# A hybrid encoder block in three-matmul f32: eight products in some projection pieces, a residual added by the store, one more step ahead of a broadcast

## The chip, the cores and the metric

The kernel runs on one core of a Trainium2 chip. The metric is the time of one execution on the device in microseconds (us), lower is better. The engines are named as in the profile: PE is TensorE (matmul), PEld its weight loads, DVE is VectorE, ACT ScalarE, POOL GpSimd and SP SyncE. SP and ACT issue plain DMAs; POOL issues the DMAs that add to their destination.

## The reference, cut to what matters

The input is 512 tokens of 2048 features in f32.

```
hn = rmsnorm(h, g_mix); proj = hn @ w_in + b_in       # q k v o i f, cb cc ch, gm gc
hm = mlstm_chunkwise(q, k, v, i, f); ...; y_m = hm @ w_branch_m        # 1024 -> 2048
y_c = (cb * causal_dwconv(cc * ch)) @ w_branch_c                       # 1024 -> 2048
h  = h + (sigmoid(gm) * y_m + sigmoid(gc) * y_c) @ w_out               # 2048 -> 2048
hn = rmsnorm(h, g_ffn)
u  = causal_dwconv(hn @ w_up, w, b); gate, val = split(u)              # 2048 -> 2 x 5504
h  = h + (silu(gate) * val) @ w_down                                   # 5504 -> 2048
return rmsnorm(h, g_out)
```

## The kernel before, in words

Everything is held with features on the partitions and tokens along the row. An f32 product is made of three matmuls: each operand is split into a high part (ACT rounds it, `wh` for weights, `act[:, :NW]` for inputs) and a low part (DVE subtracts, `wl` and `act[:, NW:]`), and `three` in `cell_mm` issues high by high, high by low, low by high (L229, L230, L231).

The unit of work is an **item**: two blocks of 128 output features for all 512 tokens. Its sum over the input features goes in **pieces** of four 128-feature blocks, and a piece in two **cells**. A cell multiplies two by two weight blocks with two by two input blocks (two feature blocks, two halves of 256 tokens) by Winograd's form of Strassen's scheme: seven block products in place of eight, on sums of blocks. So a cell is 21 matmuls and a piece 42, each with 256 columns. The seventh product goes into bank 3 (`P_BANK`), which both items in flight share by halves, the other six into three banks of the item's set.

The sums cost work. Of a piece's weights, `fill` (L195) loads two blocks again and lets POOL add a third to each while loading (L204), and DVE makes two more sums (`s2` L169, `s4` L174). So a piece loads 512 KB plain, two plain copies of 128 KB, and adds two of 128 KB. ACT then makes two `wh` (`hi`, L184) and DVE two `wl` (`lo`, L188), 896 columns each. The inputs' seven slots are made by `cell_task` (L257): DVE sums L276, L281, L286, then high (L290) and low (L293), 1792 columns. When an item ends, `evac_first` (L245, ACT) takes bank 3's half into a buffer `z`, `evac_ops` (L251 to L254, DVE) puts the products together in it, and the item's `post` finishes it.

The phases follow one another: the input projection (40 items of 4 pieces), yc (8 items of 2 pieces), ym (8 of 2), out (8 of 4), up (43 of 4), down in three parts of its input features (8 items of 4, 3 and 3 pieces), and a short last part with plain products and the final norm. The first two and the last two items of a phase are interleaved piece by piece. One piece is one **step** of the main loop, and the program is written out step by step on all engines: in step s PE multiplies piece s, while DVE and ACT make the low and high parts of pieces s+1 and s+2 and the cells that `cells_at` puts there. A cell belongs to a whole phase, so at a phase's start four to eight new cells have to be made at once, beside the weights.

`post` work is put into a queue with a cost and is taken when the running `credit` of the step allows it; `flush(n)` forces what is still queued for items up to n. At an item's end the loop calls `flush(it.num - 3)`, then `evac_first`, and, when the item has a `pre` (a load of 512 KB for its post), `flush(it.num - 2)` and the load on SP. There are three buffers `z`, taken in turn (the order's names z_91, z_92, z_93), so `evac_first` of item n waits until the store of item n-3 has read its buffer.

In down, each part's `pre` loads the pair of h blocks, `residual` (L694, L695, DVE) adds and subtracts the sums, and ACT's queue stores the pair (L146), going from h_d to h2_d, back to h_d, and to h2_d. At out's end the squares' sum over features is made by `sum_tokens` (PE), `cols_post` (DVE, ends with L370) turns it into a diagonal, and `rows_pe` (PE, L373) broadcasts it over the partitions; these are queued as `side` stages, one per step: PE's part of a stage comes after the step's matmuls, its `post` part in the next step, ahead of that step's matmuls.

Of the kernel before, what the change touches and what calls it, by code (L numbers as in the profile page):

```python
# [49 lines left out]
class Item:  # L50


    def __init__(self, load, nq, xs, post, pre=None):
        self.load, self.nq, self.xs, self.post, self.pre = load, nq, xs, post, pre
        self.p1_start, self.urgent, self.done = True, False, False
        self.set = self.num = self.z = self.buf = None

# [11 lines left out]
def tile_block(ctx: ExitStack, tc: tile.TileContext, xT, w1, w_v0, w_v1, w_v2, w_bm, w_bc, w_out, w_up, w_down,  # L69
# [62 lines left out]
    gm_d, gc_d, mc_d, h_d, h2_d = (D_([KD, P, T], s) for s in ("gm_d", "gc_d", "mc_d", "h_d", "h2_d"))  # L132
# [16 lines left out]

    def pair_ap(d, a, b):  # L150

        return d[a:b + 1:b - a].rearrange("j p t -> p j t")
# [4 lines left out]

    def weight_task(it, q):
        t = Task(None, None, None, None)
# [46 lines left out]
    def tiles_load(w, n1, n2, k0=0):  # L206
        def load(raw, q):
            fill(raw, [w[n, :, k0 + 4 * q + i:k0 + 4 * q + i + 2, :] for n in (n1, n2) for i in (0, 2)])
# [12 lines left out]
    def cell_mm(it, q, r, t):  # L221
# [4 lines left out]
        def three(ps, ws, xs, start):  # L226
# [4 lines left out]
            PE.matmul(ps, l, xh, start=False, stop=last, skip_group_check=True)  # L231

        def p1():
            three(P_BANK[:, it.set * H2:(it.set + 1) * H2], *P1, first and it.p1_start)
# [22 lines left out]
    def cell_task(xs, c, d, scale=None, key=None):  # L257
# [7 lines left out]
        def load():  # L265
            new_raw()
            SP.dma_start(t.raw[:, 5 * SW:], d[k1])
            SP.dma_start(t.raw[:, :2 * SW], d[k2])

        def t3():  # L270
            x = slots(t.raw)
            if scale:
                A.activation(t.raw[:, 5 * SW:], t.raw[:, 5 * SW:], AF.Copy, scale=scale(k1))
                A.activation(t.raw[:, :2 * SW], t.raw[:, :2 * SW], AF.Copy, scale=scale(k2))
# [13 lines left out]
        def hi():  # L288
            t.act = actp.tile([P, 2 * NW], F32R, tag="act", name=nm("act"))
            A.activation(t.act[:, :NW], t.raw, AF.Copy)  # L290

        def lo():
            V.tensor_sub(t.act[:, NW:], t.raw, f(t.act[:, :NW]))  # L293
# [4 lines left out]
        t.load, t.sums, t.hi, t.lo, t.new_raw = load, [t3, e, t4], hi, lo, new_raw  # L298
        t.cost = (1.35, 1.95)
# [3 lines left out]
    def direct_cell(xs, c, it, d=None, scale=None, key=None):  # L303

        t = cell_task(xs, c, d, None, key)
# [9 lines left out]
        def t3():  # L315
            assert it.done
            a, b = t.raw[:, 5 * SW:], t.raw[:, :2 * SW]
# [11 lines left out]
        t.cost = (2.7, 1.95) if d is not None else t.cost  # L329
# [369 lines left out]
    def out_post(p):  # L699
        def post(it):  # L700
# [8 lines left out]
            def two_():  # L709
# [610 lines left out]
```

## Time and profile before

| | |
|---|---|
| three timed runs: median (lowest to highest) | 2734.19 us (2729.54 to 2740.98) |
| the profiled execution's own time | 2736.55 us |
| its span in the trace | 2734.8 us |
| PE, DVE, ACT, POOL busy | 94%, 81%, 47%, 31% |
| mean granted clock of PE | 0.978 |
| moved by DMA | 632.39 MB, mean 231 GB/s |

The PE matmuls of the page are pipelined, so their busy times overlap; the number of matmuls in a stretch says more. In the windows view each row is a stretch in us from the span's start, then its length, and for each engine the busy time and, in brackets, the number of instructions; then the granted clock, the DMA engines' mean busy share (packets overlap, so it can pass 1) and GB/s. The phases begin at 927.4 us (yc), 1035.3 (ym), 1131.4 (out), 1311.6 (up) and, for down's three parts, 2216.2, 2403.0 and 2538.0.

### The profile page before, as it was taken

The numbers are of one execution on the slowest core, as the hardware profiler recorded it, in microseconds if no ns is written. First come the engines' busy times: TensorE is split into PE (matmuls) and PEld (weight loads), VectorE is DVE, ScalarE is ACT, GpSimd is POOL, SyncE is SP. The second block draws the span as 40 slices with busy tenths as digits, with TensorE's granted clock in tenths as the row PEclk, the third lists the DMA queues.
The fourth block names the chain that finished last, engine by engine and source line by source line (L and its number), as shares of the span: only waits on it lengthen the run. The fifth ranks groups of instructions, "written<-read, shape, count | busy, mean of one in ns | idle before, by whom it ended". The sixth has DMA issues, their size and how long they took to land.

```text
span 2734.8 us, 55343 instructions
## 1 busy us (share of the span) xinstructions
PE 2582.4 (94%) x20860; PEld 2555.7 (93%) x20860; DVE 2214.5 (81%) x3376; ACT 1289.4 (47%) x1615; POOL 854.5 (31%) x1003
## 2 busy tenths in 40 slices
PE   7899999999999978899799999999999988989898
PEld 6899999999999978899699999999999988989897
DVE  5677776887677889978779988888888888787876
ACT  6444544445554434345545444444444444444443
POOL 3243333333333222232233333333333323232320
PEclk9999999999999999999899999999999999999998
DMA  7799988898999889898698888988888789899996
GB/s 191 176 235 234 242 230 225 218 240 235 239 238 228 229 252 268 227 269 242 181 226 212 227 220 220 229 217 226 219 221 227 204 217 263 234 288 260 275 266 200
DMA packets 499036, 632.39 MB, mean 231 GB/s; under 512 B 46496, under 2 KB 327072, under 8 KB 498768
## 3 DMA queue, kind: packets, MB, share of 16 engines
q1 hardware_dynamic: 323472, 446.01, 51.4%
q0 software_dynamic: 141536, 125.09, 31.0%
q10 hardware_dynamic: 33760, 57.76, 5.8%
q8 instruction: 163, 2.67, 0.4%
q14 instruction: 105, 0.86, 0.1%
HBM read 571.01 MB, written 57.67 MB: 230 GB/s over the span
## 4 chain that ended last, share of the span: by engine, by line
PE 75%; DVE 9%; DMA 7%; issue 3%; ACT 1%; POOL 0%; SPq 0%; DVEq 0%; ACTq 0%; POOLq 0%
PE bank L231 24%; PE bank L229 24%; PE bank L230 24%; DVE wl L188 3%; DMA raw<-in_w_down_dram 2%; DMA raw<-in_w_bc_dram 1%; DVE act L293 1%; DMA raw<-in_w_out_dram 1%; DMA h_d<-z 1%; DVE raw L169 1%; PE bank L542 1%; DMA raw<-in_w_up_dram 1%; DVE z L252 1%; DVE z L251 0%; DVE raw L174 0%
## 5 line engine op out<-in xcount | busy, mean ns | idle before, releaser
L231 PE MATMUL bank<-act,wl 128*128 128x256 f32 x6664 | 1909.4, 287 | 66.6 <-DVE wl L188 66.5
L229 PE MATMUL bank<-act,wh 128*128 128x256 f32 x6664 | 1915.7, 287 | 34.1 <-ACT z L245 19.0
L230 PE MATMUL bank<-act,wh 128*128 128x256 f32 x6664 | 1902.5, 285 | 0.6 <-DVE act L293 0.5
L184 ACT ACTIVATE wh<-raw 128x896 fp32r<-128x896 f32 x952 | 893.8, 951 | 1144.9 <-PE bank L230 715.6
L231 PEld LDWEIGHTS bank<-act,wl 128*128 128x128 f32 x6664 | 1296.6, 195 | 76.5 <-DVE wl L188 76.2
L229 PEld LDWEIGHTS bank<-act,wh 128*128 128x128 f32 x6664 | 1297.2, 195 | 40.7 <-ACT z L245 20.6
L230 PEld LDWEIGHTS bank<-act,wh 128*128 128x128 f32 x6664 | 1296.7, 195 | 4.3 <-issue 2.0
L188 DVE TENSOR_TENSOR wl<-raw,wh 128x896 fp32r<-128x896 f32 x952 | 1034.2, 1087 | 222.3 <-PE bank L231 156.1
L204 POOL DMA_DIRECT2D raw<-in_w_up_dram x344 | 299.3, 963 | 606.9 <-DMA raw<-in_w_up_dram 266.3
L204 POOL DMA_DIRECT2D raw<-in_w_dram x288 | 250.7, 944 | 550.6 <-DMA raw<-in_w_dram 300.4
L169 DVE TENSOR_TENSOR raw<-raw 128x256 f32<-128x256 f32 x476 | 199.6, 419 | 55.5 <-DMA raw<-in_w_down_dram 22.1
L204 POOL DMA_DIRECT2D raw<-in_w_down_dram x160 | 139.4, 973 | 309.3 <-DMA raw<-in_w_down_dram 119.8
L174 DVE TENSOR_TENSOR raw<-raw 128x256 f32<-128x256 f32 x476 | 199.0, 418 | 0.2
L290 ACT ACTIVATE act<-xraw 128x1792 fp32r<-128x1792 f32 x52 | 88.3, 1697 | 91.2 <-DVE xraw L286 91.1
L251 DVE TENSOR_TENSOR z<-bank,z 128x512 f32<-128x512 f32 x131 | 89.9, 686 | 19.2 <-ACT z L245 17.4
L293 DVE TENSOR_TENSOR act<-xraw,act 128x1792 fp32r<-128x1792 f32 x52 | 105.0, 2019 | 0.0
L584 DVE TENSOR_TENSOR z<-z,rstd 128x1024 f32<-128x1024 f32 x83 | 101.1, 1219 | 0.0
L204 POOL DMA_DIRECT2D raw<-in_w_out_dram x64 | 55.7, 966 | 125.8 <-DMA raw<-in_w_out_dram 91.5
L252 DVE TENSOR_TENSOR z<-bank,z 128x512 f32<-128x512 f32 x131 | 89.7, 684 | 0.8 <-DVE z L251 0.5
L254 DVE TENSOR_TENSOR z<-bank,z 128x512 f32<-128x512 f32 x131 | 89.6, 684 | 0.0
L245 ACT ACTIVATE z<-bank 128x256 f32<-128x256 f32 x131 | 48.2, 368 | 25.6 <-DMA h_d<-z 11.5
L253 DVE TENSOR_TENSOR z<-bank,z 128x256 f32<-128x256 f32 x131 | 55.6, 425 | 4.5
(208 smaller groups left out, 1209.6 us busy)
## 6 DMA issues: line engine op xcount, KB each, us to landing
raw<-in_w_up_dram SPq DMA_DIRECT2D x172, 512.0 KB, 5.9
raw<-in_w_dram SPq DMA_DIRECT2D x144, 512.0 KB, 5.8
raw<-in_w_up_dram SPq DMA_DIRECT2D x344, 128.0 KB, 4.4
raw<-in_w_up_dram POOLq DMA_DIRECT2D x344, 128.0 KB, 5.2
raw<-in_w_down_dram SPq DMA_DIRECT2D x80, 512.0 KB, 6.2
raw<-in_w_dram SPq DMA_DIRECT2D x288, 128.0 KB, 4.1
raw<-in_w_dram POOLq DMA_DIRECT2D x288, 128.0 KB, 5.2
raw<-in_w_down_dram SPq DMA_DIRECT2D x160, 128.0 KB, 4.7
```

Source lines behind the costliest of these rows:

```text
L169: V.tensor_add(x[:, 6], x[:, 5], x[:, 0])
L174: V.tensor_add(x[:, 2], x[:, 6], x[:, 1])
L184: A.activation(seven(t.wh[r]), half(r), AF.Copy)
L188: V.tensor_sub(seven(t.wl[r]), half(r), seven(f(t.wh[r])))
L204: G.dma_start(at(i), a21, accum_op=ALU.add)
L229: PE.matmul(ps, h, xh, start=start, stop=False, skip_group_check=True)
L230: PE.matmul(ps, h, xl, start=False, stop=False, skip_group_check=True)
L231: PE.matmul(ps, l, xh, start=False, stop=last, skip_group_check=True)
L251: return [lambda: V.tensor_add(z[:, 0:4:3], b0, two(z[:, 1])), lambda: V.tensor_add(z[:, 1:3], b1, two(z[:, 3])), lambda: V.tensor_add(z[: ...
L252: lambda: V.tensor_add(z[:, 1:3], b1, two(z[:, 3])),
L293: V.tensor_sub(t.act[:, NW:], t.raw, f(t.act[:, :NW]))
L584: V.tensor_mul(sb_pair(it.z), sb_pair(it.z), two(rstd))
```

## The change

Three edits.

**Eight products.** The last piece of each item of yc, ym and out (24 pieces) goes with the eight plain block products instead of seven: `eight_task` loads only the 512 KB, makes no sums, and takes high and low parts in 256-column halves, of 512 columns in all for each cell (the second output block with its sign turned, since the item's second half is kept negative). PE makes 48 matmuls for such a piece. The inputs of these pieces need six slots, made by one difference in place of three sums. As the shared bank gets nothing from that piece, its group of sums ends a piece earlier (`p1_end`). The costs that the planner reckons with are lower for them.

**Down's residual.** down's items have no `pre`. The post turns the second block's sign on ACT and the store becomes a DMA of POOL that adds the pair to h_d in place. h2_d is gone. The post's cost in the planner goes from 1.3 to 0.1.

**One more step.** A stage that does nothing stands between the squares' sum and the broadcast ahead of up.

```diff
+    def add_to(dst, src, key):
+        def fn():
+            G.dma_start(dst, src, accum_op=ALU.add)
+            stored.add(key)
+        late.append(fn)
...
+    def eight_task(it, q):
...
+        def hi(r):
+            w = t.wh[r] = wp.tile([P, NC], F32R, tag="wh", name=nm("wh"), bufs=4)
+            A.activation(at(w, 0), blk(0, r), AF.Copy)
+            A.activation(at(w, 1), blk(1, r), AF.Copy, scale=-1.0)
+
+        def lo(r):
+            w = t.wl[r] = wp.tile([P, NC], F32R, tag="wl", name=nm("wl"), bufs=3)
+            V.tensor_sub(at(w, 0), blk(0, r), at(f(t.wh[r]), 0))
+            V.scalar_tensor_tensor(at(w, 1), blk(1, r), -1.0, at(f(t.wh[r]), 1), op0=ALU.mult, op1=ALU.subtract)
...
+        t.load, t.sums, t.hi, t.lo = load, [], hi, lo
+        t.cost = (0, 1.5)
...
-            fill(raw, [w[n, :, k0 + 4 * q + i:k0 + 4 * q + i + 2, :] for n in (n1, n2) for i in (0, 2)])
+            if not eight:
+                fill(raw, [w[n, :, k0 + 4 * q + i:k0 + 4 * q + i + 2, :] for n in (n1, n2) for i in (0, 2)])
...
+        if q == it.eight:
+            for k in range(2):
+                for ws, xs, b, half in ((k, 2 * k, 0, 0), (k, 2 * k + 1, 2, 0), (2 + k, 2 * k + 1, 1, 1), (2 + k, 4 + k, 2, 1)):
+                    three(SETS[it.set][b][:, half * H2:(half + 1) * H2], ws, xs, False, last and k == 1)
+            return
...
-        t.load, t.sums, t.hi, t.lo, t.new_raw = load, [t3, e, t4], hi, lo, new_raw
-        t.cost = (1.35, 1.95)
+        t.load, t.sums, t.hi, t.lo, t.new_raw = load, [diff] if eight else [t3, e, t4], hi, lo, new_raw
+        t.cost = (0.65, 1.7) if eight else (1.35, 1.95)
...
                     side.append((lambda: sum_tokens(SIDE, acc, 1, 4, True, True), cols))
+                    side.append((noop, noop))
                     side.append((rows_pe, rows_post))
...
             def fn():
-                residual(it)
-                store(pair_ap((h2_d, h_d, h2_d)[c], j1, j2), sb_pair(it.z), ("d", c, p))
-            return [(1.3, fn)]
+                b = it.z[:, T:]
+                A.activation(b, b, AF.Copy, scale=-1.0)
+                add_to(pair_ap(h_d, j1, j2), sb_pair(it.z), ("d", c, p))
+            return [(0.1, fn)]
...
-            pre = load_pair((h_d, h2_d, h_d)[c], *kpair(p))
-            items.append(Item(tiles_load(w_down, *kpair(p), k0), nq, AA, down_post(c, p), pre))
+            items.append(Item(tiles_load(w_down, *kpair(p), k0), nq, AA, down_post(c, p)))
```

The orders of three places before and after follow, as the programs have them: line, operation, what is written from what, and its shape.

DVE in yc, where the third item's second piece gets its low parts (`wl`; `z` rows are an item's end, `raw` rows sums of weights), before:

```order
L169 TENSOR_TENSOR raw_10784<-raw_10784 128x256
L251 TENSOR_TENSOR z_92<-bank_84,z_92 128x2x256
L174 TENSOR_TENSOR raw_10784<-raw_10784 128x256
L252 TENSOR_TENSOR z_92<-bank_85,z_92 128x512
L253 TENSOR_TENSOR z_92<-bank_85,z_92 128x256
L188 TENSOR_TENSOR wl_10996<-raw_10778,wh_10918 128x896
L254 TENSOR_TENSOR z_92<-bank_86,z_92 128x512
L188 TENSOR_TENSOR wl_10999<-raw_10778,wh_10975 128x896
L169 TENSOR_TENSOR raw_10908<-raw_10908 128x256
L188 TENSOR_TENSOR wl_11049<-raw_10784,wh_10993 128x896
L174 TENSOR_TENSOR raw_10908<-raw_10908 128x256
L188 TENSOR_TENSOR wl_11054<-raw_10784,wh_11043 128x896
```

The same place on DVE now:

```order
L210 TENSOR_TENSOR raw_10767<-raw_10767 128x256
L301 TENSOR_TENSOR z_92<-bank_84,z_92 128x2x256
L215 TENSOR_TENSOR raw_10767<-raw_10767 128x256
L302 TENSOR_TENSOR z_92<-bank_85,z_92 128x512
L303 TENSOR_TENSOR z_92<-bank_85,z_92 128x256
L188 TENSOR_TENSOR wl_10987<-raw_10765,wh_10909 128x256
L189 SCALAR_TENSOR_TENSOR wl_10987<-raw_10765,wh_10909 128x256
L304 TENSOR_TENSOR z_92<-bank_86,z_92 128x512
L188 TENSOR_TENSOR wl_10991<-raw_10765,wh_10969 128x256
L189 SCALAR_TENSOR_TENSOR wl_10991<-raw_10765,wh_10969 128x256
L737 TENSOR_TENSOR z_91<-z_91,mA 128x1024
L229 TENSOR_TENSOR wl_11042<-raw_10767,wh_10984 128x896
```

Two subtractions of 896 columns, the first two `wl` rows of the upper list, became four of 256 (L188 and L189 in the lower), and the sums of the next such piece (L169 and L174 between the last `wl` rows of the upper list) are gone; yc's post (L737) has moved up into that place.

ACT in down's third part, from the end of its first item to the end of its third, before. `L245` is `evac_first`, `L184` makes a `wh` (two a step), and `L146` is a store, which goes out here in the order of ACT's queue:

```order
L146 DMA h_d<-z_91 128x2x512
L184 ACTIVATE wh_29367<-raw_29177 128x896
L184 ACTIVATE wh_29379<-raw_29183 128x896
L245 ACTIVATE z_91<-bank_83 128x256
L146 DMA h_d<-z_92 128x2x512
L184 ACTIVATE wh_29434<-raw_29183 128x896
L184 ACTIVATE wh_29446<-raw_29242 128x896
L184 ACTIVATE wh_29496<-raw_29242 128x896
L184 ACTIVATE wh_29508<-raw_29248 128x896
L184 ACTIVATE wh_29554<-raw_29248 128x896
L184 ACTIVATE wh_29566<-raw_29306 128x896
L245 ACTIVATE z_92<-bank_83 128x256
```

ACT at the same place now; `L813` is the sign turned ahead of POOL's add of the same buffer, `L295` is `evac_first`, `L225` makes a `wh`:

```order
L813 ACTIVATE z_91<-z_91 128x512
L295 ACTIVATE z_91<-bank_83 128x256
L225 ACTIVATE wh_29481<-raw_29236 128x896
L225 ACTIVATE wh_29493<-raw_29295 128x896
L225 ACTIVATE wh_29543<-raw_29295 128x896
L225 ACTIVATE wh_29555<-raw_29301 128x896
L225 ACTIVATE wh_29601<-raw_29301 128x896
L813 ACTIVATE z_92<-z_92 128x512
L813 ACTIVATE z_93<-z_93 128x512
L813 ACTIVATE z_91<-z_91 128x512
L225 ACTIVATE wh_29616<-raw_29359 128x896
L295 ACTIVATE z_92<-bank_83 128x256
```

The store of z_91 stood two `wh` ahead of the `evac_first` that writes the buffer anew, that of z_92 seven rows ahead; now the sign of z_91 is turned in the row just ahead of it, and that of z_92 four rows ahead, and the add comes after that. Without a `pre`, `flush(it.num - 2)` no longer forces the older item's post out at the item's end.

DVE at the start of down's first part, from the end of up's last posts but one: `L584` to `L743` are an up post, before:

```order
L743 TENSOR_TENSOR mB<-mB 128x512
L169 TENSOR_TENSOR raw_25837<-raw_25837 128x256
L251 TENSOR_TENSOR z_92<-bank_84,z_92 128x2x256
L174 TENSOR_TENSOR raw_25837<-raw_25837 128x256
L252 TENSOR_TENSOR z_92<-bank_85,z_92 128x512
L253 TENSOR_TENSOR z_92<-bank_85,z_92 128x256
L188 TENSOR_TENSOR wl_25991<-raw_25773,wh_25918 128x896
L254 TENSOR_TENSOR z_92<-bank_86,z_92 128x512
L188 TENSOR_TENSOR wl_25994<-raw_25773,wh_25976 128x896
L584 TENSOR_TENSOR z_91<-z_91,rstd 128x1024
L734 SCALAR_TENSOR_TENSOR mA<-z_91,pcol,mA 128x511
L735 SCALAR_TENSOR_TENSOR mA<-z_91,pcol,mA 128x510
```

There on DVE now, from the same post's end (L802 was L743) on:

```order
L802 TENSOR_TENSOR mB<-mB 128x512
L210 TENSOR_TENSOR raw_25926<-raw_25926 128x256
L301 TENSOR_TENSOR z_93<-bank_80,z_93 128x2x256
L215 TENSOR_TENSOR raw_25926<-raw_25926 128x256
L302 TENSOR_TENSOR z_93<-bank_81,z_93 128x512
L303 TENSOR_TENSOR z_93<-bank_81,z_93 128x256
L229 TENSOR_TENSOR wl_26136<-raw_25920,wh_26060 128x896
L304 TENSOR_TENSOR z_93<-bank_82,z_93 128x512
L229 TENSOR_TENSOR wl_26139<-raw_25920,wh_26121 128x896
L210 TENSOR_TENSOR raw_25985<-raw_25985 128x256
L229 TENSOR_TENSOR wl_26192<-raw_25926,wh_26133 128x896
L215 TENSOR_TENSOR raw_25985<-raw_25985 128x256
```

up's last two posts stood in two steps that follow one another; now the first of them comes one step later and the second four steps later.

More of the change, by code (lines that the diff above doesn't have):

```diff
@@ L131, in tile_block @@
     so_d, cb_d, yc_d, hm_d = (D_([8, P, T], s) for s in ("so_d", "cb_d", "yc_d", "hm_d"))
[L132 removed]
+    gm_d, gc_d, mc_d, h_d = (D_([KD, P, T], s) for s in ("gm_d", "gc_d", "mc_d", "h_d"))
     a_d = D_([NF, P, T], "a_d")
@@ L224, in cell_mm, with three @@
         first, last = c == 0, c == 2 * it.nq - 1
-        def three(ps, ws, xs, start):
+        def three(ps, ws, xs, start, stop=last):
             h, l = (w[r][:, ws * P:(ws + 1) * P] for w in (t.wh, t.wl))
@@ L266, in load, with two_k, diff @@
             new_raw()
-            SP.dma_start(t.raw[:, 5 * SW:], d[k1])
-            SP.dma_start(t.raw[:, :2 * SW], d[k2])
+            for dst, k in zip(t.two(), (k1, k2)):
+                SP.dma_start(dst, d[k])
+        def two_k():
+            return (t.raw[:, :T], t.raw[:, T:2 * T]) if eight else (t.raw[:, 5 * SW:], t.raw[:, :2 * SW])
+        def diff():
+            x = slots(t.raw)
+            V.tensor_sub(x[:, 4:6], x[:, 0:4:2], x[:, 1:4:2])
         def t3():
@@ L316, in t3 @@
             assert it.done
-            a, b = t.raw[:, 5 * SW:], t.raw[:, :2 * SW]
+            a, b = t.two()
             if d is not None:
```

58 lines of the change are left out of this document (38 added, 20 removed).

## The prediction

> **What bounds the kernel now.** I read the page's busy times first, then the busy times of each engine by stretches, then in each stretch that isn't full what its engine waits for. From the page, the engines and the three large queues (packets, MB, share of 16 DMA engines):
>
> ```profile
> PE 2582.4 (94%) x20860; PEld 2555.7 (93%) x20860; DVE 2214.5 (81%) x3376; ACT 1289.4 (47%) x1615; POOL 854.5 (31%) x1003
> ...
> q1 hardware_dynamic: 323472, 446.01, 51.4%
> q0 software_dynamic: 141536, 125.09, 31.0%
> q10 hardware_dynamic: 33760, 57.76, 5.8%
> ```
>
> The stretches of the change, from the windows view (yc, ym, out, up's first four steps, up into down, and three of down):
>
> ```profile
> 927.40:1035.30 107.90, 88.84 (x672) 87.21 (x673) 92.03 (x131) 43.34 (x50) 31.06 (x36) 0.92 0.90 252
> 1035.30:1131.40 96.10, 85.11 (x674) 83.89 (x673) 89.01 (x131) 39.12 (x44) 23.11 (x27) 0.96 0.92 261
> 1131.40:1311.60 180.20, 166.83 (x1346) 164.39 (x1345) 149.48 (x220) 83.80 (x93) 55.22 (x64) 0.98 0.91 245
> 1311.60:1357.60 46.00, 29.67 (x179) 27.77 (x180) 34.35 (x57) 22.76 (x27) 10.46 (x12) 0.74 0.58 150
> 2216.20:2299.80 83.60, 68.64 (x504) 66.61 (x505) 70.42 (x100) 35.86 (x40) 26.87 (x32) 0.92 0.89 229
> 2395.60:2451.80 56.20, 48.32 (x380) 47.10 (x379) 49.36 (x72) 23.85 (x26) 18.58 (x22) 0.97 1.00 279
> 2451.80:2522.40 70.60, 70.60 (x591) 70.60 (x590) 56.40 (x86) 30.04 (x33) 22.03 (x26) 1.00 0.99 283
> 2522.40:2588.70 66.30, 55.98 (x423) 54.62 (x422) 56.89 (x82) 27.35 (x29) 20.92 (x24) 0.92 0.96 265
> ```
>
> The seventh row is PE with nothing in its way: 70.60 us for 591 matmuls, 0.12 us each, so a step of 42 has a floor of 5.04. Against it yc's 672 matmuls could take 80.6 and took 107.9 (27.3 lost), ym's 80.6 of 96.1 (15.5 lost), out's 1346 some 161.5 of 180.2 (18.7 lost), and up's four steps 20.2 of 46.0 (25.8 lost). What yc waits for stands in DVE's groups of that stretch (busy, mean ns of one, idle before them):
>
> ```profile
> L188 DVE TENSOR_TENSOR wl<-raw,wh 128x896 fp32r<-128x896 f32 x34 | 36.9, 1084 | 2.2 <-PE bank L231 2.0 <-issue 0.2
> L293 DVE TENSOR_TENSOR act<-xraw,act 128x1792 fp32r<-128x1792 f32 x6 | 12.1, 2019 | 0.0
> L174 DVE TENSOR_TENSOR raw<-raw 128x256 f32<-128x256 f32 x17 | 7.1, 418 | 0.0
> L169 DVE TENSOR_TENSOR raw<-raw 128x256 f32<-128x256 f32 x16 | 6.7, 421 | 10.2 <-DMA raw<-in_w_bc_dram 10.2
> ```
>
> DVE is busy 92.0 us and idle 12.4 before these groups, 104.4 of 107.9: DVE bounds yc, with PE 11 us of work behind it once 48-matmul pieces are counted below. In ym DVE has 89.0 of 96.1.
>
> **Eight products.** PE: 24 pieces of 48 matmuls for 42 add 144, 17.3 us at 0.12. DVE, per piece: two `wl` of 1.084 and the sums of 0.421 and 0.418 go, 3.01 us; four subtractions of 256 columns come, which I take at the 0.42 of L174's 256 columns, 1.68. A piece saves 1.33, and a phase's eight 10.6. A cell with six slots saves two 256-column sums (0.42 each) and a seventh of 2.019: 1.1. It loads 512 KB where a piece loaded 1 MB, and POOL issues two adds fewer.
>
> In yc fall its own two such cells and ym's two (their places are −6 and −3 ahead of ym): 10.6 + 4.4 = 15.0 off a DVE that is the bound. PE's floor rises to 80.6 + 8 × 0.72 = 86.4, so the most to win is 21.5. I take −14: DVE's 15.0, less 1 where PE, only 6 us below DVE by then, is late itself. If only half of DVE's relief reaches the end, −7; if the 10.2 us of transfer wait go too (a quarter of the weight bytes are gone), −21.
>
> In ym DVE loses 10.6 and stands at 78.4, below PE's 86.4: PE is the bound then, and −9.7 the most. Out, whose DVE is free for 30 us, still loses a tenth of its floor, so I leave 4 us of loss in ym: −5.7 (0 to −9.7).
>
> In out PE has 167.3 as its floor, and DVE, at 149.5, isn't the bound on the mean; its loss sits at the start, where cells are made, and at the end. Taking a phase's 18.7 of loss to about 8 (two cells with six slots at the start, no sums for each item's last piece, where the item's end falls as well) gives 175.3: −5. If the losses stay as they are but for 3, it is +3; if they go, −12.
>
> **One more step.** From the table of waits (total, times, longest), and DVE's timeline behind PE's wait:
>
> ```profile
> ACT z L245 <- DMA h_d<-z: 11.5, 2, 6.1
> ...
> PE bank L373 <- DVE mC L370: 10.6, 1, 10.6
> ```
>
> ```profile
> 1355.31 1.09 DVE L188 TENSOR_TENSOR wl<-raw,wh 128x896 fp32r<-128x896 f32 x1 [4.68 <-PE bank L231]
> ```
>
> PE stood 10.6 us at the broadcast with a step's matmuls behind it; then DVE stood 4.68 for those. A step later, PE does 5.04 us of matmuls in that wait, and DVE's 4.68 goes: −5. In these 46 us the granted clock is 0.74, so a shorter hole also wins part of 0.26 × 46 = 12; for that and DVE's shorter work for out's last pieces I take −5 more. −10, between −4 (the broadcast is waited for again, only later) and −16 (nearly all but the cells' work goes). Nothing waits for the broadcast but up's first posts, an item's four steps later.
>
> **Down's residual, at up's end.** DVE's timeline, the first row of each of two up posts that the flush forces out, and the last of the second:
>
> ```profile
> 2263.59 1.22 DVE L584 TENSOR_TENSOR z<-z,rstd 128x1024 f32<-128x1024 f32 x1
> ...
> 2274.32 1.22 DVE L584 TENSOR_TENSOR z<-z,rstd 128x1024 f32<-128x1024 f32 x1
> ...
> 2279.51 0.69 DVE L743 TENSOR_TENSOR mA<-mA 128x512 f32<-128x512 f32 x1
> ```
>
> A post is 5.9 us of DVE (2274.32 to 2280.20), and DVE's step with it 10.7 (2263.59 to 2274.32) where PE's floor is 5.04, two steps running, in a stretch of 0.92 clock. The order now spreads the two over more steps. The rest of these steps' work stays (an item's end, the next phase's cells), so I take −3; 0 if DVE is as late without them, −8 if most of the two steps' 11.4 over the floor goes.
>
> **Down's residual, in down.** DVE loses 48 sums, each under the 1.22 of L584's double width, ACT gains 24 sign turns, POOL 24 issues, and SP loses 24 loads ahead of weights. On POOL the add waits for the turn, with the next weights' adds queued behind; POOL is idle 37.6 of 56.2 in the sixth row. All of it lies on engines that leave PE full (70.60 of 70.60 with DVE 56.4, ACT 30.0, POOL 22.0): nothing; were that cover gone, a turn of under an `L184`'s 0.95 ahead of each item's `wh` would cost up to 23. What costs is the buffer. ACT's rows at two item ends of before, ACT's and POOL's, and the landing times (KB, median us):
>
> ```profile
> 2434.43 0.45 ACTq L146 DMA_DIRECT2D h_d<-z  x1
> 2434.99 0.95 ACT L184 ACTIVATE wh<-raw 128x896 fp32r<-128x896 f32 x1 [1.52 <-PE bank L231]
> 2437.00 0.95 ACT L184 ACTIVATE wh<-raw 128x896 fp32r<-128x896 f32 x1 [1.06 <-DVE z L252]
> 2443.37 0.39 ACT L245 ACTIVATE z<-bank 128x256 f32<-128x256 f32 x1 [5.41 <-DMA h_d<-z]
> ```
>
> ```profile
> 2569.16 0.45 ACTq L146 DMA_DIRECT2D h_d<-z  x1
> 2569.72 0.95 ACT L184 ACTIVATE wh<-raw 128x896 fp32r<-128x896 f32 x1 [1.13 <-PE bank L231]
> 2571.67 0.95 ACT L184 ACTIVATE wh<-raw 128x896 fp32r<-128x896 f32 x1 [1.00 <-PE bank L230]
> 2578.75 0.38 ACT L245 ACTIVATE z<-bank 128x256 f32<-128x256 f32 x1 [6.12 <-DMA h_d<-z]
> ```
>
> ```profile
> 2438.02 0.86 POOL L204 DMA_DIRECT2D raw<-in_w_down_dram  x1 [0.25 <-issue]
> ```
>
> ```profile
> raw<-in_w_down_dram SPq DMA_DIRECT2D x160, 128.0 KB, 4.7
> raw<-in_w_down_dram POOLq DMA_DIRECT2D x160, 128.0 KB, 5.8
> raw<-in_w_out_dram SPq DMA_DIRECT2D x32, 512.0 KB, 5.8
> h_d<-z ACTq DMA_DIRECT2D x32, 512.0 KB, 5.6
> ```
>
> The stores there took 8.9 and 9.6 us until `evac_first` could write the buffer, and ACT stood 5.41 and 6.12 with every further `wh` queued behind it. Now the sign is turned later, and the add waits on POOL's queue behind the weights' adds. How long an add of 512 KB takes no row shows. A small add takes 5.8 where a small copy takes 4.7; by that ratio 8.9 to 9.6 become 11 to 11.8, and I take 11; bounds 5.8 (as a small one) and 14.
> Second part's second item: the add goes out at about 2437.5, between POOL's issues; 2448.5 against 2443.37: +5.1. Third part's second item: the turn stands just ahead of `evac_first`, behind the last `wh` at 2571.67, so the add goes at about 2573.8: 2584.8 against 2578.75: +6.0. Third part's third item: the turn comes one step ahead of `evac_first`, which waited for nothing before: 11 + 0.8 for turn and issue − 5.04 = +6.8, and 1.7 of clock beside it (0.03 × 56.2 in the stretch that has one such wait). Together +19.6; with 5.8 it is +2.4, with 14 about +29. Elsewhere the turn is two steps or more ahead.
>
> **Sum**, against the profiled execution's 2736.55: −14 − 5.7 − 5 − 10 − 3 + 19.6 = −18.1, 2718.4; that run lies 2.4 above the median of the three, so 2716.
>
> **Rivals.** *Adds land like small ones.* Then the buffers cost 2.4 and the sum is −35.3: 2699. For it: a plain 512 KB lands as soon as a 128 KB add (5.8 and 5.8), and DMA is lighter now. Against: stores of 5.6 in the median took 8.9 and 9.6 at just these places. The Trainium skill's "DMA: Bandwidth & Descriptors", section "Anatomy of one DMA — SWDGE (gpsimd) path", gives 2.0 us and bytes by 436e3 for such a transfer, 3.2 for this one, by which no buffer would come later than now and the sum would be −37.7, 2696; by the same rule the adds of 128 KB take 2.3, and the trace has 5.8. Chance 0.22.
>
> *An add holds the DMA engines too long (slower).* In down they are full beside PE (0.99 and 1.00). A load and a store of 512 KB, 0.524 MB, cost them, by the queues' rows, 0.524 × 0.514 × 2734.8 / 446.01 = 1.65 and 0.524 × 0.058 × 2734.8 / 57.76 = 1.44, together 3.09. An add at q0's rate is 0.524 × 0.310 × 2734.8 / 125.09 = 3.55, little more; but q0's adds go into SBUF, and this one into DRAM, which it has to read and write. If it costs c, each of the sixteen items of three pieces is longer by c − 3.09, less the slack that the share leaves (0.04 of an item's 15.1 us by the row of 0.96, next to none by the others), some 8 us in all. It passes no change from c = 4.7; at 5.5 it is +31: 2747. Chance 0.16.
>
> *The three phases don't pay.* If DVE is idle there because transfers land late (10.2 in yc, share 0.90 to 0.92), what DVE saves becomes more waiting: yc, ym and out stay as they are and the sum is −10 − 3 + 19.6 = +6.6: 2741. Against it, 92.0 of 107.9 are work. Chance 0.10.
>
> That the change doesn't do what it says the order excludes: 24 pieces have the four short rows, and `L813` is there.
>
> **How the numbers follow.** The forecast's case has 0.52. A difference of 0.5%, 13.7 us, is about what a measurement can tell. Faster by more is below 2720.5: some 0.62 of the forecast's case (0.32) and all of the first rival (0.22): 0.54. Slower by more is above 2747.9: 0.11 of the second rival and 0.01 of the forecast's: 0.12. The rest 0.34. The range 2690 to 2742 takes in the first and third rivals, and the unknown landing time from 5.8 to 14; out of it lie most of the second, and a tail.
>
> **What would show it.** In the profile after: yc near 94 us, ym 90, out 175, with DVE's transfer wait in yc under 10; PE's wait at the broadcast under 6 and up's first four steps near 36; `evac_first`'s waits on POOL's add in the second part's second and third part's second and third items, 8 to 12 us each; the add's landing time in the DMA rows (11, against 5.8 or 14); DMA share and PE in down's middle stretch still full. Wrong I am if yc, ym and out together win under 12, if `evac_first` waits at other items too, or if PE is no longer full in 2451 to 2522's steps.

## The result, and the profile after

| | before | changed |
|---|---|---|
| median of four runs (lowest to highest) | 2735.64 us (2729.54 to 2740.98) | 2716.99 us (2714.14 to 2719.14) |
| the profiled execution, its span | 2736.55, 2734.8 us | 2714.14, 2712.4 us |
| mean granted clock of PE | 0.978 | 0.984 |

The ratio is 0.9932, with a 95% interval of 0.9908 to 0.9956: 0.7% faster, where 2716 had been forecast. The two spans differ by 22.4 us. First the page's busy times and large queues of the changed kernel:

```profile
PE 2580.9 (95%) x21004; PEld 2556.1 (94%) x21004; DVE 2149.7 (79%) x3316; ACT 1290.3 (48%) x1687; POOL 843.3 (31%) x979
...
q1 hardware_dynamic: 310032, 427.13, 49.7%
q0 software_dynamic: 141152, 131.38, 32.9%
q10 hardware_dynamic: 27232, 45.17, 4.6%
```

PE has 144 matmuls more, and its busy time isn't longer. Next the same steps as in the prediction's stretches: yc, ym, out, up's first four steps, up into down, three stretches of down, and as a ninth two steps that stood at their floor before (10.1 us):

```profile
925.30:1014.20 88.90, 86.87 (x723) 86.46 (x722) 79.50 (x124) 39.25 (x66) 15.68 (x18) 1.00 0.92 279
1014.20:1104.90 90.70, 87.43 (x723) 86.62 (x722) 79.52 (x132) 36.57 (x61) 13.98 (x16) 1.00 0.76 220
1104.90:1281.20 176.30, 169.94 (x1394) 168.74 (x1392) 134.57 (x211) 78.91 (x107) 40.42 (x47) 0.99 0.82 224
1281.20:1319.20 38.00, 26.33 (x180) 24.72 (x179) 31.95 (x54) 20.26 (x23) 10.14 (x12) 0.91 0.69 182
2175.40:2255.80 80.40, 65.22 (x504) 63.39 (x505) 65.83 (x92) 34.71 (x38) 27.22 (x32) 0.96 0.88 223
2352.90:2416.80 63.90, 49.20 (x380) 47.78 (x379) 47.59 (x69) 25.48 (x29) 24.31 (x27) 0.92 0.95 233
2416.80:2487.40 70.60, 70.60 (x591) 70.60 (x590) 49.97 (x74) 33.05 (x39) 25.73 (x28) 1.00 1.01 236
2487.40:2557.70 70.30, 56.50 (x423) 55.08 (x422) 54.52 (x78) 27.64 (x30) 24.85 (x29) 0.90 0.87 218
2557.70:2576.60 18.90, 11.62 (x86) 11.41 (x85) 7.12 (x11) 5.64 (x8) 7.46 (x8) 0.82 1.01 206
```

Row by row against before: yc 107.9 to 88.9, ym 96.1 to 90.7, out 180.2 to 176.3, up's start 46.0 to 38.0, up into down 83.6 to 80.4; then 56.2 to 63.9, 70.6 as before, 66.3 to 70.3, and 10.1 to 18.9. So the projections and up's start gave 36 us, and the three rows of down that got longer took 20.5 back.

What became of yc's waits shows in PE's groups of that stretch, before and after (busy, mean ns of one, idle before it and what ended it):

```profile
L231 PE MATMUL bank<-act,wl 128*128 128x256 f32 x224 | 66.9, 299 | 11.2 <-DVE wl L188 11.2
L229 PE MATMUL bank<-act,wh 128*128 128x256 f32 x224 | 66.6, 297 | 8.2 <-ACT z L245 6.2 <-DVE z L251 1.9
```

```profile
L273 PE MATMUL bank<-act,wl 128*128 128x256 f32 x241 | 68.4, 284 | 2.0 <-DVE wl L229 2.0
L271 PE MATMUL bank<-act,wh 128*128 128x256 f32 x241 | 68.2, 283 | 0.0
```

PE waited 19.4 us in yc before and 2.0 after. The rest of the 27.3 us that yc lost is PE working slower: by the rows of yc it was busy 88.8 us where its matmuls have a floor of 80.6, at a mean granted clock of 0.92. After, it is busy 86.9 for a floor of 86.4, at a clock of 1.00. A stretch's loss can be read so: PE's idle time (length less busy), and what its busy time has over the floor. The Trainium skill's "TensorE: Matmul & The Clock Gate", section "HAM oscillation — how this bites in real kernels", has PE fall to a lower clock at idle gaps of more than some 3.4 us. yc's two longest gaps before were 4.74 us (to 961.84) and 5.71 us (to 992.59), and the clock is low behind the first, as the first row shows; after, the longest gap is 1.43 us and the clock 1.00. So far the trace agrees; but the second row is as low behind two waits of 1.58 and 1.89 us that lie half a microsecond apart, so one gap of that length isn't needed here.

```profile
962.00:966.00 4.00, 4.00 (x22) 4.00 (x23) 3.96 (x7) 1.57 (x2) 2.14 (x3) 0.57 1.08 327
1019.00:1024.00 5.00, 5.00 (x30) 5.00 (x31) 5.00 (x7) 0.00 (x0) 1.87 (x3) 0.66 1.01 280
```

DVE's groups in yc, after, against the four that the prediction shows:

```profile
L229 DVE TENSOR_TENSOR wl<-raw,wh 128x896 fp32r<-128x896 f32 x18 | 19.4, 1085 | 3.9 <-PE bank L273 2.1 <-issue 1.8
L350 DVE TENSOR_TENSOR act<-xraw,act 128x1536 fp32r<-128x1536 f32 (+1 forms) x6 | 11.0, 1840 | 0.0
L189 DVE SCALAR_TENSOR_TENSOR wl<-raw,wh 128x256 fp32r<-128x256 f32 x16 | 6.7, 417 | 0.0
L188 DVE TENSOR_TENSOR wl<-raw,wh 128x256 fp32r<-128x256 f32 x16 | 6.7, 417 | 2.1 <-PE bank L273 1.8 <-issue 0.3
...
L210 DVE TENSOR_TENSOR raw<-raw 128x256 f32<-128x256 f32 x8 | 3.4, 420 | 2.0 <-DMA raw<-in_w_bc_dram 2.0
```

DVE's wait for transfers went from 10.2 to 2.0, and what it waits for now is PE: the bound has changed sides, as the prediction had it for ym, but in yc too.

In down, the three places of the prediction, first on ACT (start, length, and in brackets the wait before it): `L813` turns the sign, `L295` is `evac_first`.

```profile
2390.90 1.13 ACT L813 ACTIVATE z<-z 128x512 f32<-128x512 f32 x2
...
2406.30 0.38 ACT L295 ACTIVATE z<-bank 128x256 f32<-128x256 f32 x1 [12.54 <-DMA h_d<-z]
...
2535.51 0.62 ACT L813 ACTIVATE z<-z 128x512 f32<-128x512 f32 x1
2547.84 0.39 ACT L295 ACTIVATE z<-bank 128x256 f32<-128x256 f32 x1 [11.71 <-DMA h_d<-z]
...
2558.68 1.65 ACT L813 ACTIVATE z<-z 128x512 f32<-128x512 f32 x3
...
2571.89 0.38 ACT L295 ACTIVATE z<-bank 128x256 f32<-128x256 f32 x1 [10.60 <-DMA h_d<-z]
```

The adds on POOL's queue that belong to them, and their landing time in the DMA rows (median us):

```profile
2399.02 3.15 POOL L154 DMA_DIRECT2D h_d<-z  x2
...
2539.73 1.56 POOL L154 DMA_DIRECT2D h_d<-z  x1
...
2562.66 4.02 POOL L154 DMA_DIRECT2D h_d<-z  x3
```

```profile
h_d<-z POOLq DMA_DIRECT2D x24, 512.0 KB, 8.8
```

A row with x2 or x3 holds several turns or adds; the buffer that `evac_first` waits for is the first of them. From its turn's start to its add's issue pass 8.1, 4.2 and 4.0 us (7.0, 3.6 and 2.3 from the end of the row of turns), from there to `evac_first` 7.3, 8.1 and 9.2. Behind `evac_first` stand ACT's further `wh`, and PE: the steps that begin there (the first of the third item in the second part, and of the third and fourth in the third part) lose 11.8, 10.6 and 8.9 us over their 5.04, where before they lost 2.4, 4.5 and none.

### The profile page after: what moved, and what is told of

It is laid out like the page before. It is cut to its first block, busy times and chain, and to the rows that moved or that the text cites. A ratio compares the mean times of both kernels' runs of the same rounds, so it can differ in the third digit from the quotient of the medians.

```text
span 2712.4 us, 55375 instructions
## 1 busy us (share of the span) xinstructions
PE 2580.9 (95%) x21004; PEld 2556.1 (94%) x21004; DVE 2149.7 (79%) x3316; ACT 1290.3 (48%) x1687; POOL 843.3 (31%) x979
## 3 DMA queue, kind: packets, MB, share of 16 engines
q0 software_dynamic: 141152, 131.38, 32.9%
## 4 chain that ended last, share of the span: by engine, by line
PE 48%; DVE 7%; DMA 7%; issue 3%; ACT 1%; POOL 0%; SPq 0%; DVEq 0%; POOLq 0%; ACTq 0%
PE bank L273 16%; PE bank L271 16%; PE bank L272 15%; DMA raw<-in_w_down_dram 4%; DVE wl L229 2%; DVE act L350 1%; DMA h_d<-z 1%; DMA raw<-in_w_up_dram 1%; DMA raw<-in_w_out_dram 1%; PE bank L420 0%; PE bank L1095 0%; DVE raw L210 0%; DVE z L302 0%; PE bank L1096 0%; PE bank L1097 0%
## 5 line engine op out<-in xcount | busy, mean ns | idle before, releaser
L225 ACT ACTIVATE wh<-raw 128x896 fp32r<-128x896 f32 x904 | 849.0, 951 | 1055.0 <-PE bank L272 712.9
L229 DVE TENSOR_TENSOR wl<-raw,wh 128x896 fp32r<-128x896 f32 x904 | 981.2, 1087 | 235.8 <-PE bank L273 158.5
L245 POOL DMA_DIRECT2D raw<-in_w_up_dram x344 | 299.1, 954 | 616.1 <-DMA raw<-in_w_up_dram 275.0
L245 POOL DMA_DIRECT2D raw<-in_w_dram x288 | 251.0, 952 | 550.0 <-DMA raw<-in_w_dram 312.1
L245 POOL DMA_DIRECT2D raw<-in_w_down_dram x160 | 143.5, 1017 | 291.5 <-DMA raw<-in_w_down_dram 152.6
L210 DVE TENSOR_TENSOR raw<-raw 128x256 f32<-128x256 f32 x452 | 189.4, 419 | 40.1 <-DMA raw<-in_w_down_dram 21.4
L215 DVE TENSOR_TENSOR raw<-raw 128x256 f32<-128x256 f32 x452 | 188.6, 417 | 0.2
L347 ACT ACTIVATE act<-xraw 128x1792 fp32r<-128x1792 f32 (+1 forms) x52 | 87.0, 1672 | 81.8 <-DVE xraw L343 75.0
L350 DVE TENSOR_TENSOR act<-xraw,act 128x1792 fp32r<-128x1792 f32 (+1 forms) x52 | 103.3, 1987 | 0.0
L245 POOL DMA_DIRECT2D raw<-in_w_out_dram x48 | 41.9, 996 | 129.5 <-DMA raw<-in_w_out_dram 61.1
L295 ACT ACTIVATE z<-bank 128x256 f32<-128x256 f32 x131 | 48.2, 368 | 45.6 <-DMA h_d<-z 34.8
```

What stands on the lines that cost most here:

```text
L210: V.tensor_add(x[:, 6], x[:, 5], x[:, 0])
L215: V.tensor_add(x[:, 2], x[:, 6], x[:, 1])
L225: A.activation(seven(t.wh[r]), half(r), AF.Copy)
L229: V.tensor_sub(seven(t.wl[r]), half(r), seven(f(t.wh[r])))
L245: G.dma_start(at(i), a21, accum_op=ALU.add)
L350: V.tensor_sub(t.act[:, NW:NW + m], t.raw[:, :m], f(t.act[:, :m]))
```

## The experiments

Each kernel was timed against the kernel before on the same chip; its ratio is that to before. The changed kernel's own is 0.9932, so only ratios, and stretches of the profile, are compared across.

### Each edit undone

**Old residual, the rest as changed.**

```diff
-                A.activation(b, b, AF.Copy, scale=-1.0)
-                add_to(pair_ap(h_d, j1, j2), sb_pair(it.z), ("d", c, p))
+                residual(it)
+                store(pair_ap((h2_d, h_d, h2_d)[c], j1, j2), sb_pair(it.z), ("d", c, p))
```

> The changed kernel with down's old residual put back (load of the pair, two sums on DVE, plain store); eight products and the further step stay. Theory (the add costs only by its landing, through the z buffers): against the changed kernel the three waits at the ends of down's items 1 and 2 go, down's second and third part together get 21 us shorter, the first part about 3 longer: 2699 us, 0.987 of before. Rival (the pair's loads and stores weigh on full DMA engines, and the add relieves them): no faster than the changed kernel, 2717 or more.

Measured: 2694.61 us, 0.9863 (0.9847 to 0.988). Down's second and third part take 133.0 and 129.4 us, against 142.2 and 145.7 in the changed kernel. The stretch from up into down takes 84.1 against 80.4. The two parts here, then in the kernel before:

```profile
2364.30:2497.30 133.00, 124.44 (x1008) 122.82 (x1008) 113.33 (x169) 57.38 (x62) 41.88 (x49) 0.99 0.99 279
2497.30:2626.70 129.40, 123.82 (x1009) 122.81 (x1009) 108.01 (x159) 53.20 (x61) 38.26 (x44) 0.99 0.97 273
```

```profile
2403.00:2538.00 135.00, 124.42 (x1008) 122.79 (x1008) 113.54 (x169) 57.39 (x62) 41.56 (x48) 0.99 0.97 273
2538.00:2669.30 131.30, 125.86 (x1008) 125.11 (x1009) 108.26 (x159) 53.22 (x61) 38.35 (x44) 0.96 0.96 269
```

`evac_first`'s waits for a transfer, in the table of waits, first the changed kernel, then this one:

```profile
ACT z L295 <- DMA h_d<-z: 34.8, 3, 12.5
```

```profile
ACT z L295 <- DMA h_d<-z: 10.9, 2, 5.4
```

So this edit costs the changed kernel 19 us net by the ratios, 22 by the medians; the other two edits alone are worth 1.4%. The rival falls: with the pair's loads and stores back, down is faster.

**Seven products everywhere, the rest as changed**; of the edit, ym's lines (yc and out go the same way):

```diff
-    ym_items = [Item(tiles_load(w_bm, *kpair(p)), 2, HM, ym_post(p), load_pair(gm_d, *kpair(p)), 1) for p in range(8)]
-    phase(ym_items, HM, [cell_task(HM, c, hm_d, None, [("hm", k) for k in kpair(c)], c > 1) for c in range(4)],
+    ym_items = [Item(tiles_load(w_bm, *kpair(p)), 2, HM, ym_post(p), load_pair(gm_d, *kpair(p))) for p in range(8)]
+    phase(ym_items, HM, [cell_task(HM, c, hm_d, None, [("hm", k) for k in kpair(c)]) for c in range(4)],
```

> The changed kernel with seven products everywhere. Theory (the eight products win because DVE bounds yc and ym): yc back to about 107, ym to 96, out to 180, together 28 us longer, 2745 us, 1.004 of before; down as in the changed kernel. Rival (yc got shorter by another order of the posts or of what went before): yc stays under 98 and the kernel is under 2732.

Measured: 2744.73 us, 1.0051 (1.003 to 1.0071). yc's stretch:

```profile
929.20:1038.60 109.40, 90.11 (x675) 88.19 (x674) 91.86 (x130) 43.44 (x50) 31.35 (x36) 0.91 0.92 252
```

yc 109.4, ym 95.0, out 179.1: within 1.5 us of before the change, and the whole is slower than before. The gain in the three phases is the eight products'. They also give something where they aren't: two steps of up that lose 3.5 and 4.1 us in the kernel before and in this one lose 1.6 each in every kernel here with eight products in all three phases (the credit that the planner brings into up differs; that this is the cause is only argued).

**Without the empty stage, the rest as changed.**

```diff
                     side.append((lambda: sum_tokens(SIDE, acc, 1, 4, True, True), cols))
-                    side.append((noop, noop))
```

> The changed kernel without the empty stage ahead of up's broadcast. Theory (PE does a step's matmuls in the wait for the broadcast): PE's wait there is 9 to 11 us again where the changed kernel has 3.3, up's start is 8 to 10 us longer, 2726 us. Rival (the shorter DVE work of out's last pieces made up's start shorter): PE's wait stays under 6 and the time within 3 us of the changed kernel.

Measured: 2723.01 us, 0.9969 (0.9959 to 0.9979). PE's wait at the broadcast, first the changed kernel, then this one:

```profile
L431 PE MATMUL bank<-mC,ones 128*128 128x512 f32 x2 | 1.5, 838 | 3.3 <-DVE mC L428 3.3
```

```profile
L431 PE MATMUL bank<-mC,ones 128*128 128x512 f32 x2 | 2.1, 1138 | 10.6 <-DVE mC L428 10.6
```

The wait is 10.6 again, and up takes 899.0 us for 894.2: 4.8 us in the trace, less than the 8 to 10 expected; the ratios lie 10 us apart, with some 7 of uncertainty on the changed kernel's. The loss of up's first four steps is 25.3 here and was 25.8 before the change. In the changed kernel it is 17.9, but its fifth and sixth steps lose 2.9, and here nothing. So the stage wins 5 us at that place, and DVE's shorter work in out's last pieces wins next to nothing there.

**Seven products in out alone.**

```diff
-    out_items = [Item(tiles_load(w_out, *kpair(p)), 4, MM, out_post(p), load_pair(xT, *kpair(p)), 3) for p in range(8)]
-    phase(out_items, MM, [direct_cell(MM, c, ym_items[c], mc_d, None, [("mc", c)], c > 5) for c in range(8)],
+    out_items = [Item(tiles_load(w_out, *kpair(p)), 4, MM, out_post(p), load_pair(xT, *kpair(p))) for p in range(8)]
+    phase(out_items, MM, [direct_cell(MM, c, ym_items[c], mc_d, None, [("mc", c)]) for c in range(8)],
```

> The changed kernel with seven products in out; yc and ym keep their pieces of eight. Theory (out's losses shrink by its own pieces of eight, by more than PE's 5.8 us for them): out's loss is 17 to 19 again, out 179 us, the kernel 3 us longer than the changed one, 2720. Rival (out's start was late because of what yc and ym left undone, and the pieces of eight only cost in out): out's loss stays at 9 to 10, out is 171, the kernel 6 us shorter, 2711.

Measured: 2719.18 us, 0.9957 (0.9943 to 0.9971). Out's stretch:

```profile
1104.20:1283.80 179.60, 168.57 (x1347) 166.93 (x1345) 146.74 (x215) 83.36 (x91) 54.21 (x63) 0.96 0.90 244
```

179.6 for 176.3, as expected, with 18.3 us of loss for 9.3. The ratios are 7 us apart and their intervals overlap: the phase shows it, the time alone wouldn't. The pieces of eight win in out too, where DVE isn't the bound on the mean.

### What the eight products win by

**Bytes put back**: the pieces of eight load what pieces of seven load; nothing reads the rest.

```diff
-            it.load(t.raw, q, True)
+            it.load(t.raw, q)
```

> The changed kernel, whose pieces of eight products load what a piece of seven loads: two plain copies and two of POOL's adds more, which nothing reads. DVE, ACT and PE have the work of the changed kernel. Theory (DVE's relief made yc and ym shorter): yc and ym stay within 3 us of the changed kernel's 88.9 and 90.7, the time is 2717 to 2722. Rival (fewer bytes and fewer of POOL's adds made them shorter): yc is over 98 and the time over 2728.

**DVE's time put back**: two sums that nothing reads.

```diff
+        def extra():
+            V.tensor_add(t.raw[:, 4 * SW:6 * SW], t.raw[:, :2 * SW], t.raw[:, 2 * SW:4 * SW])
-        t.load, t.sums, t.hi, t.lo = load, [], hi, lo
+        t.load, t.sums, t.hi, t.lo = load, [extra, extra], hi, lo
```

> The changed kernel, whose pieces of eight products get two more sums on DVE, of 512 columns, into slots that nothing reads: 1.37 us of DVE a piece, about what the eight products save it (1.33). Loads, ACT and PE have the work of the changed kernel. Theory (DVE's relief made yc and ym shorter): yc's DVE goes from 79.5 to 90.5 us and yc to about 99, ym to about 97, out 2 to 4 longer: 2736 us, about as before. Rival (the transfers): yc and ym stay within 3 us of 88.9 and 90.7 and the time is under 2724.

**Both put back**, by the two edits above in one kernel.

> The changed kernel, whose pieces of eight both load what a piece of seven loads and get the two more sums of 512 columns on DVE; nothing reads either. Theory (DVE's work and its waits for transfers come one after the other in yc, so each alone was hidden in part by what the other left free): yc goes from 88.9 to 103 to 107, ym to 97, more than the 6.6 + 4.4 and 4.0 + 3.8 that the two kernels with one of them added, and the time is 2742 to 2750, above the kernel before, since PE's 144 matmuls stay. Rival (the two simply add): yc 99.9, ym 98.5, 2737.

Measured: bytes 2727.72 us, 0.9987 (0.9977 to 0.9997); DVE's time 2726.31, 0.9983 (0.9972 to 0.9995); both 2734.82, 1.0014 (1.0002 to 1.0027). yc's stretch in each, in this order, and PE's waits in the last:

```profile
927.00:1022.50 95.50, 88.18 (x720) 86.85 (x721) 79.05 (x125) 39.77 (x67) 31.00 (x36) 1.00 1.00 289
```

```profile
928.50:1021.70 93.20, 87.80 (x722) 86.71 (x721) 88.88 (x142) 39.43 (x67) 15.71 (x18) 1.00 0.88 260
```

```profile
925.40:1022.00 96.60, 90.97 (x720) 89.49 (x721) 88.39 (x141) 39.64 (x67) 30.96 (x36) 0.96 0.99 288
```

```profile
L276 PE MATMUL bank<-act,wl 128*128 128x256 f32 x240 | 70.0, 292 | 5.6 <-DVE wl L188 3.5 <-DVE wl L232 2.1
L274 PE MATMUL bank<-act,wh 128*128 128x256 f32 x240 | 69.2, 288 | 1.4 <-DVE z L304 1.4
```

No theory holds as stated. Bytes alone bring back 6.6 us in yc and 4.0 in ym (the DMA engines' share goes from 0.92 to 1.00), DVE's time alone 4.4 and 3.8: neither is nothing, neither is all. Both together give 7.7 and 7.0, nearly the sum in ym and less in yc, not the more-than-sum that waits in series would give. In ym that is more than the whole gain: 97.7 us, where seven products take 95.0 with fewer matmuls. But yc's 96.6 is still 12.8 short of the 109.4 that it takes with seven products. A part of DVE's time isn't back: it is busy 88.4 us in yc here and 91.9 with seven products, since the cells keep their six slots. What else stays away is seen in PE's waits: before, 8.2 us of them were for an item's end (`L245`, `L251`), here 1.4; and DVE's two added sums wait for no add of POOL, since they read only the plain load. The diff has a reason for each (bank 3's sums end a piece earlier by `p1_end`; the chain load, add, sum, high part is two links shorter), but no kernel put these or the cells' slots back alone, so their shares stay open.

### What holds down's buffers

**Five z buffers**: mA and mB, free in down now, join from down's second part on; first in the turn mA, mB, z2, z0, z1, in which the last part writes over the last item's buffer before its add has gone out; then as here:

```diff
                 it.z = zs[it.set] if it.num < 40 else (z2, zs[0], zs[1])[(it.num - 40) % 3]
+                if it.num >= 115:
+                    it.z = (z2, mA[:, :2 * T], mB[:, :2 * T], zs[0], zs[1])[it.num % 5]
```

> The changed kernel with five z buffers in turn in place of three in down's second and third part (mA and mB, which down no longer uses, join). Theory (evac_first waits only for the add that still reads its buffer): the waits of 12.5, 11.7 and 10.6 us go, and with them the loss of steps 434, 458 and 461 (11.8 + 10.6 + 8.9 less the 2 to 4 that the item's end had else), 22 to 29 us less: 2692, 0.984 of before. Rival (the DMA engines bound these steps, and the waits only show it): weights come late in their place, and at most 8 us are won, 2709.

> As the kernel with five z buffers, in another turn, so that the last part writes no buffer whose add is still to be issued (there the last item's add had read what the last part wrote over it). Theory: the time of that kernel, 2689 us, 0.984 of before; no evac_first waits for an add of POOL. Rival (the last items' adds, kept in order, hold up the last part): 2 to 6 us more, 2693.

Measured: 2688.71 us, 0.9838 (0.9823 to 0.9852), and 2687.34 us, 0.9842 (0.9828 to 0.9857). Down's second and third part in the changed kernel, then in the second of these:

```profile
2359.30:2501.50 142.20, 126.35 (x1009) 124.94 (x1009) 104.55 (x153) 60.98 (x71) 51.66 (x56) 0.95 0.96 229
2501.50:2647.20 145.70, 126.70 (x1009) 125.48 (x1010) 97.60 (x141) 58.30 (x71) 49.24 (x53) 0.94 0.89 212
```

```profile
2364.10:2494.80 130.70, 125.48 (x1009) 124.33 (x1009) 104.64 (x153) 61.18 (x71) 51.54 (x56) 0.97 1.01 250
2494.80:2621.50 126.70, 123.38 (x1009) 122.57 (x1010) 97.43 (x141) 58.15 (x71) 49.30 (x53) 0.99 0.99 243
```

In down no `evac_first` waits for a transfer any more, and the two parts are 30.5 us shorter. By the rows PE's idle time (length less busy) falls from 34.9 to 8.5 us, 26.3 of the 30.5, which leaves some 4 for PE's clock. The mean granted clock overstates that part: 0.95 to 0.97 and 0.94 to 0.99 of the lengths would be 11 us, but some of the low clock falls into the wait itself, as in this row of the changed kernel:

```profile
2401.40:2406.60 5.20, 0.00 (x0) 0.00 (x0) 0.00 (x0) 0.30 (x2) 2.59 (x3) 0.50 1.12 174
```

So the add's cost was the buffer, and no loss of that size comes in its place. With buffers enough, the add looks a little better than the old residual: 257.4 us against 262.4 for the two parts in the trace, 0.9842 against 0.9863 in time, with intervals that overlap.

**POOL's adds as plain copies.** This kernel leaves down's earlier parts out of its sum.

```diff
-            G.dma_start(dst, src, accum_op=ALU.add)
+            G.dma_start(dst, src)
```

> The changed kernel with POOL's adds of down made plain copies of the same size from the same queue: down's earlier parts are left out of the sum that it gives. Theory (an add lands much like a copy; it comes late because the turn and POOL's queue are late): the landing stays at 7.5 to 9 us in the median, evac_first's three waits at 10 us or more, the time at 2712 to 2718. Rival (adding in DRAM, which reads and writes there, is what takes long): the landing falls to 6.5 or less, the waits by 2 to 3 us each, the time to 2709 or less.

Measured: 2713.40 us, 0.9941 (0.9919 to 0.9964). Its landing, its `evac_first` waits, and its row of POOL's queue:

```profile
h_d<-z POOLq DMA_DIRECT2D x24, 512.0 KB, 6.6
```

```profile
ACT z L295 <- DMA h_d<-z: 32.8, 3, 12.0
```

```profile
q0 software_dynamic: 138080, 131.38, 31.2%
```

The landing goes from 8.8 to 6.6, about what the rival said, but the three waits only from 34.8 to 32.8 in all, as the theory said: at these places a copy comes nearly as late as an add. On the DMA engines, 32.9% of 2712.4 us less 31.2% of 2711.2 is 46.5 us for 24 transfers, so an add takes 1.9 us more of all 16 engines than a copy. The kernel with the old residual, which has neither in this queue, gives an add's whole cost: 32.9% of 2712.4 less 30.2% of 2692.4 is 79.3 us, 3.3 an add.

```profile
q0 software_dynamic: 134624, 118.80, 30.2%
```

**The add issued at once.**

```diff
-        def fn():
-            G.dma_start(dst, src, accum_op=ALU.add)
-            stored.add(key)
-        late.append(fn)
+        G.dma_start(dst, src, accum_op=ALU.add)
+        stored.add(key)
```

> The changed kernel with each of down's adds issued on POOL right where its sign turn is issued on ACT, ahead of the next step's adds for weights, not behind them. Theory (part of the wait is POOL's order: from the turn to the add's issue are 7 us at step 434, 3.6 at 458 and 2 at 461): evac_first's waits get shorter by these, 9 to 12 us in all, 2706. Rival (POOL then stands at the turn with the weights' adds behind it, and weights come late): at most 3 us won, 2714 or more.

Measured: 2712.85 us, 0.9938 (0.9917 to 0.9959). `evac_first`'s waits:

```profile
ACT z L293 <- DMA h_d<-z: 28.2, 3, 12.3
```

They are 10.4, 12.3 and 5.5 for 12.5, 11.7 and 10.6: 6.6 us less in all, 5.1 of it at the third place. Down's two parts take 282.8 us for 287.9; the ratio can't be told from the changed kernel's. That lies between the theory's 9 to 12 and the rival's 3. At the first place the add now goes out 3.1 us after its turn's start for 8.1, but takes 9.9 us from there to `evac_first` for 7.3; at the second it still stands behind adds for weights (4.4 for 4.2). So POOL's order is a part of the wait, and the landing, together with what POOL still waits for ahead of the add, the larger one.

**Two empty stages**, on the five buffers.

```diff
                     side.append((noop, noop))
+                    side.append((noop, noop))
```

> The kernel with five z buffers in its second form, with one more empty stage ahead of up's broadcast, so two. Theory (what is left of PE's wait for the broadcast, 3.3 us, goes too): 3 us less, 2684. Rival (PE is held in step 227 by its low parts, and DVE's work to be done there stays the same): within 1.5 us of 2687.

Measured: 2684.92 us, 0.9841 (0.9815 to 0.9867), the ratio of the kernel with one (0.9842); the interval is too wide to tell 3 us. PE's wait at the broadcast is gone, and up's first six steps lose what they lost: 20.7 us here, 20.8 in the changed kernel (5.0 in the fifth step for 1.9, 3.8 in the fourth for 6.4). The wait has moved, not gone: by the steps the rival holds.

## Why the prediction was right, and where it was off

The time (2716 for 2717) and the sum (−18.1 for −22.4 in the spans) held, with some luck in the sum: yc won 5 us more than its term and up's start 5 less. Term by term:

- **yc −14: −19.0.** Mis-sized, inside its −7 to −21. The term counted DVE's work alone. PE's 27.3 us of loss were 19.4 of waits and 8 of clock, and all but 2.5 went: with the waits went the clock's share, and PE's 8.2 us of waits for an item's end, which the step "DVE bounds yc" had not priced. That step had counted DVE's 10.2 us of waiting for transfers as DVE's bound, and its 11 us of PE "behind" are DVE's 92.0 less a floor of 42-matmul pieces; with pieces of 48 they are 5.6. The reason that the prediction gave is only a part of the cause: 11 us of DVE's time put back in yc give 4.4.
- **ym −5.7: −5.4**, and PE is the bound there, as said. **Out −5: −3.9**, with 9.3 us of loss left for the 8 assumed.
- **Up's start −10: −8.0 in its first four steps (38.0 us, where 36 was to be seen), but −5 for the stage,** since 2.9 come back in the next two. The first −5, PE's step of matmuls in the wait, was right. The second, for clock and DVE's shorter work, was wrong: without the stage, the first four steps lose 25.3 for 25.8. That the whole of up is shorter by 10.3 is chance: 5 more came from two later steps and up's end.
- **Up into down −3: −3.2.** The flush and its two posts were priced rightly: with the old residual put back the stretch takes 84.1 us.
- **Buffers +19.6: +24.4 at the three places**, 9.5, 6.0 and 8.9 for 5.1, 6.0 and 8.5, and +21.6 in the two parts as a whole. The places and the mechanism were right. The split was not: the add lands in 7.3 to 9.2 us, not 11, but goes out 3 to 5 us later than reckoned, behind POOL's adds for weights. The two errors work against each other, and that the term came so near is in part luck.
- **Nothing for DVE, SP, POOL and ACT in down**: the middle stretch is at 70.60 of 70.60 as before.

The rivals. *Adds land like small ones*: no, 8.8 us. The estimate of 3.2 us for such a transfer by the Trainium skill's fit ("DMA: Bandwidth & Descriptors", section "Anatomy of one DMA — SWDGE (gpsimd) path") is not met here, even by POOL's plain copy (6.6), in stretches with a DMA share of 0.87 to 1.01. *An add holds the DMA engines too long*: it costs 3.3 us for the 3.09 of the load and store, well under the 4.7 from which it would have decided. *The three phases don't pay*: they paid 28 us, though its ground was in part right, since bytes put back alone cost 13.5 us in the three phases.

## What to carry to other kernels

A transfer that takes over an engine's work holds its buffer from the last write to its landing, and that time, with the issue's place in its queue, has to fit between two uses of the buffer: count the buffers first, above all those that the change itself sets free. Price a stretch's loss as the tensor engine's idle time and what its busy time has over the floor: in yc 17 us of waits went, and 8 us of slower matmuls with them. The mean granted clock times the length counts too much where the low clock falls into the wait. Here two of three edits win 37 us and the third costs about 20; the sum alone, a small gain, doesn't tell it, and undoing each does.

## What the runs showed of the hardware that was not expected

- An add of 512 KB from SBUF into DRAM takes 1.9 us more of all 16 DMA engines than a plain copy by the same queue, and lands in 8.8 us in the median against 6.6.
- At the three places in down, in stretches with a DMA share of 0.87 to 1.01, that difference hardly shows: the longest wait for it was 12.5 us with adds and 12.0 with copies.
- Of the 27.3 us that yc lost, 8 were PE working slower (busy 88.8 us for a floor of 80.6, granted clock 0.92). Of the 30.5 that five buffers won in down, only some 4 were, though the mean granted clocks would give 11: the clock stood at 0.50 in 5.2 us in which PE had nothing to do.
